# Four edits to a fused decoder layer on one core: another buffer for samples' states, an output tile issued earlier, weights split by one engine, and an end written out by hand

## Chip, core and metric

The kernel runs on one core of one Trainium2 chip. The metric is the device time of one execution in microseconds; lower is better. Before the change the median of three runs is 1122.03 us (1121.79 to 1123.79). The engines of the core are named as in the profile: PE is TensorE (matrix products), PEld its loading of weights, DVE is VectorE, ACT is ScalarE, POOL is GpSimd and SP is SyncE, which here does nothing but issue transfers.

## What is computed

One layer of a hybrid decoder in float32, for 512 tokens of one prompt and for 8 samples of 8 tokens each, with shared weights and a model width of 1024. The core of the reference:

```python
u = _rms(x) * g_pre_mix
z, xbc, dt_raw, q, k, v, ig, fg, og = jnp.split(u @ w_in, split_at, axis=-1)
xbc, conv_new = causal_conv(xbc, conv_buf, conv_w, conv_b)
...
y_ssd, h_new = ssd_scan(xs, dt, a, bm, cm, h_ssm)            # 16 heads, state 64 x 128 each
...
h_ml, c_new, n_new, m_new = mlstm_scan(q, k, v, i_pre, logf, mc, mn, mm)   # 4 heads, state 128 x 256
mix = jnp.concatenate([y_ssd, h_ml], axis=-1) @ w_out
x = x + _rms(mix) * g_post_mix
# cross-attention over 256 memory rows
x = x + _rms(o) * g_post_x
f = (jax.nn.silu(u @ w_gate) * (u @ w_up)) @ w_down          # hidden width 2816
x = x + _rms(f) * g_post_ffn
```

`_rms` divides by the root of the mean square plus 1e-6. The prompt starts from empty states; each sample brings its own states (`h0` for the SSD heads, `c0` for the mLSTM heads) and its own cached memory keys and values. Outputs are the layer's result (prompt and samples), the memory keys and values, and all states after the step.

## The kernel before

**Precision.** TensorE multiplies float32 in a reduced form, so every weight tile is split in two: `split_w` (L173) loads a 128x1024 piece `raw`, ScalarE casts it to `whi` (L181), and a low part `wlo = raw - whi` follows. Columns below `cut` are subtracted by VectorE (L188); those above go to GpSimd, either by a subtraction or, with `acc`, by ScalarE writing `-whi` into `wlo` (L185) and a transfer that GpSimd issues and that adds the raw weights from memory on top (L186). Each product is then three matmuls (L201 high by high, L202 high by low activation, L203 low weight by high activation). `raw` has two buffers, `whi` and `wlo` three each.

**Layout and stages.** Activations lie with features on the partitions and 576 tokens (512 prompt, 64 sample) along the free axis, in eight tiles of 128 features. The token axis is worked in two halves, 0 to 255 (`HALVES[0]`) and 256 to 575. The stages follow each other on TensorE: input projection (with the SSD scan and the mLSTM woven into it), values, gates, output projection, cross-attention, gated feed-forward, down projection.

**Who sets the order.** From the start to the output projection the framework's scheduler orders the instructions of each engine from their dependences and from the memory that tiles take and give back; `issue_after` adds a dependence by hand. Each engine works through its own queue in order; SP's queue holds most loads and the stores. From the cross-attention on a plan is written out by hand: functions are put at positions (`at_(position, function)`, L1424), sorted, and issued in that order on all engines (L1820 to L1822).

**Samples' SSD states (L651 to L735).** In four rounds `b`, two samples' states `h0` (128x1024) are loaded by SP (L714), read by eight products `ps_hs` (L718), scaled by `decs` on GpSimd (L725), updated from `ps_hu` (L728) by VectorE (L729) and stored (L731). They share the tag `t4` with the short-lived tiles `xdts` and `xes`: three buffers of 4 KB in a partition.

**Samples' mLSTM states (L897 to L925).** The same for `c0` in two groups of four samples: load (L912), four products `ps_nh` for the heads (L914) behind four of the group's own term (L907), update from `ps_cu` (L921), store (L924); again three buffers `t4`.

**Values (L756 to L794).** `gemm_tok` multiplies tokens by `wv` for the four heads, two weight pieces each; its third matmul is L777. It calls `split_w` with `acc`, so the upper 512 columns of the eight low parts come by L185 and L186. The results go to `vt4`, which takes all of slot 2 of the large buffers.

**Mixer's second half and output projection (L988 to L1150).** After the gates ScalarE and VectorE write the split of the mLSTM's half of the mixer's output (`mixm_h`, `mixm_l`) in eight tiles. The output projection runs in two passes: the first (`ps_o1`) over the SSD half, `mixs_h`, eight tiles; the second over `mixm_h`.

**The end (L1860 to L1918).** The down projection's last third is worked for half 1 of the tokens first, then for half 0 in eight tiles of 18 matmuls `ps_dn`. `down_evac` adds a tile to `f2` (VectorE, L1863), squares it (ScalarE, L266), adds the square to `ssqf` (VectorE, L267) and scales it (L1865). When half 1 is through, its inverse root mean square is formed (`rstd_cols`, L220: sums over the partitions by products with ones, L226; then on VectorE L236, a power on GpSimd L237, and a Newton step L238 to L240), spread to rows, applied to `f2`, added to the residual `x2` and stored (L1918). For half 0, `final0` transposes the residual (`ps_xt`) and `f2` (`ps_ft`) to token rows, both by L1876, copies the first to SBUF (L1884), and adds the scaled second: three of the four parts by VectorE (L1898), one by ScalarE and GpSimd (L1895, L1896). SP stores each part (L1899). In `final0` the order of TensorE alone is written by hand; other engines are left to the scheduler. L2020 is the end of the program: each engine's closing `DRAIN` and a barrier over all engines.

Of the kernel before, what the change touches and what calls it, by code (L numbers as in the profile page):

```python
# [19 lines left out]
P = 128  # L20
T = 576
# [95 lines left out]
def build(nc, tc, ctx, I, O):  # L117
# [178 lines left out]
    wz = ml.tile([P, 256], BF16, name="wz")  # L296
# [35 lines left out]
    st = ExitStack()  # L332
    sp = st.enter_context(tc.tile_pool(name="startp", bufs=1, reuse_waits="tile"))
# [48 lines left out]
    cdup = bcp.tile([16, 2, TS], F32, name="cdup")  # L382

# [182 lines left out]
    def ssd_prompt(g):  # L566
# [34 lines left out]
        for j in range(4):  # L601
# [3 lines left out]
            for k in range(2):  # L605
# [3 lines left out]
                lm = ml.tile([P, 512], F32, name="lm", tag="tmp", bufs=2)  # L609
# [70 lines left out]
    decs = sd.tile([P, 16, NB], F32, name="decs")  # L680
# [30 lines left out]
    for b in range(4):  # L711
        hns = [sd.tile([P, 16, 64], F32, name="h0", tag="t4", bufs=3) for _ in range(2)]
# [37 lines left out]
    vt4 = SL(2, "vt4", F32, (P, 4, 4, 258))  # L750
# [41 lines left out]
    for h in range(4):  # L792
        gemm_tok(I["wv"][h], U, UL, CHUNKS, v_evac(h), True)
# [5 lines left out]
    def head_norm(num, ex, n4, pool, name):  # L799

        ss = pool.tile([P, n4], F32, name="hn_ss", tag="hn_ss", bufs=2)
        jk = pool.tile([P, 256], F32, name="hn_jk", tag="hn_jk", bufs=1)
# [20 lines left out]
    for h in range(4):  # L823
# [38 lines left out]
        f = head_norm(num, expnm[:, :, h:h + 1].rearrange("p c o -> p (c o)"), 4, mp_, "p")  # L862
# [17 lines left out]
    es = ms.tile([P, 4, TS], F32, name="es")  # L880
# [21 lines left out]
    for hb in range(2):  # L902
# [31 lines left out]
        f = head_norm(num, ex, 1, ms, "s")  # L934
        hn = ms.tile([P, 256], F32, name="hns", tag="hns", bufs=1)
        V.tensor_scalar(hn, num[:, 0, 0:256], f, None, op0=ALU.mult)
# [8 lines left out]
    def tmp():  # L945
        return ml.tile([P, 512], F32, name="tmp", tag="tmp", bufs=2)
# [42 lines left out]
    ogs = ml.tile([P, KT, TS], F32, name="ogs")  # L989
# [87 lines left out]
    f = SL(5, "f_mix")  # L1077
# [7 lines left out]
    evs, ahead = [], []  # L1085
# [23 lines left out]
    for j in range(8):  # L1109
        gemm2([(*split_w(I["wout"][j, 0], cut=1024), KT)], act(mixs_h), act(mixs_l),  # L1110
              lambda t0, n, ps: evs.append(A.copy(f[:, j, t0:t0 + n], ps)), "ps_o1")
# [760 lines left out]
    def final0():  # L1872

        def rows(src, c, d, ps):
            for j in range(4):
                m = TE.transpose(ps[:, j * P:(j + 1) * P], src[:, 4 * d + j, c * P:(c + 1) * P], ident)  # L1876
            return ps.rearrange("p (j k) -> p j k", j=4), m

        parts = [(c, d) for c in range(2) for d in range(2)]
        xr = [wp.tile([P, 2, 4, P], F32, name="raw", tag="raw", bufs=2) for _ in range(2)]  # L1880
        xt = [xr[i // 2][:, i % 2] for i in range(4)]

        def put(i):
            A.copy(xt[i], rows(x2, *parts[i], (B1 if i == 3 else GP)("ps_xt"))[0])  # L1884

        with tc.manual_schedule(engines={TE.engine}):
            for i in range(3):
                put(i)
            rc = rstd_cols([ssqf], HCHUNKS[0], "pf0", alloc=B0)
            put(3)  # L1890
            ft = [rows(f2, *parts[i], (GP if i == 3 else MP)("ps_ft"))[0] for i in range(4)]
        for i, (c, d) in enumerate(parts):
            if i == 2:
                t = sw[:, 0:512].rearrange("p (j k) -> p j k", j=4)
                A.activation(t, ft[i], AF.Copy, scale=rc[:, c:c + 1])  # L1895
                G.tensor_tensor(xt[i], xt[i], t, op=ALU.add)  # L1896
            else:
                V.scalar_tensor_tensor(xt[i], ft[i], rc[:, c:c + 1], xt[i], op0=ALU.mult, op1=ALU.add)  # L1898
            S.dma_start(O["y0"][c, :, 4 * d:4 * d + 4, :], xt[i])  # L1899


    for n_, j in enumerate(range(8)):
        ps = (MP if n_ % 2 else GP)("ps_dn")[:, :256]
# [121 lines left out]
```

## Time and profile before

| | us |
|---|---|
| median of three runs | 1122.03 |
| lowest, highest run | 1121.79, 1123.79 |
| the profiled execution | 1122.92 |
| its span in the trace | 1121.2 |
| PE busy | 1100.6 |
| DVE busy | 703.7 |
| ACT busy | 594.3 |
| POOL busy | 223.0 |

The profiled execution is one run of its own; its span runs from its first to its last instruction. The granted clock of TensorE was 0.998 over it. In the rows of the prediction `L714` is line 714 of the kernel above; `out<-in` are tiles; `x8` is a count; `[2.10 <-DMA wlo<-wv]` says that the engine stood still for 2.10 us before the instruction and what released it. A timeline's first two columns are start and duration. A group's `min/median/max` are durations in ns. In the list of waits the numbers are the total in us, how many, and the longest.

### The profile page before, as it was taken

How to read it: one execution, taken by the hardware profiler on the slowest of the kernel's cores; microseconds unless marked ns; L12 is line 12 of the kernel's file. 1: busy time of each engine (PE TensorE's matmuls, PEld its weight loads, DVE VectorE, ACT ScalarE, POOL GpSimd, SP SyncE). 2: the span in 40 equal slices, each digit the busy share in tenths (PEclk: the TensorE clock that was granted, in tenths of full speed). 3: DMA queues.
4: the chain of work that ended last, by engine and by line, in shares of the span. 5: the costliest groups of instructions: out<-in, count | busy, mean ns of one | idle time of the engine just before them, and what ended most of it. 6: DMA issues, size and time to landing. Idle time of an engine off the chain costs nothing.

```text
span 1121.2 us, 21126 instructions
## 1 busy us (share of the span) xinstructions
PE 1100.6 (98%) x8423; PEld 1049.9 (94%) x8423; DVE 703.7 (63%) x1397; ACT 594.3 (53%) x1073; POOL 223.0 (20%) x300
## 2 busy tenths in 40 slices
PE   9999999899999999999999999999999999999996
PEld 8999889798998999999988889999999999999996
DVE  6796765557786775569654455776533665447555
ACT  6877533255563465656454445556435674246543
POOL 1333544313122121000144301101001110011001
PEclk9999999999999999999999999999999999999999
DMA  6685555626564447653567855745535774357532
GB/s 208 159 165 128 134 159 159 174 68 166 146 201 107 129 144 264 226 189 104 167 223 278 282 197 170 253 114 123 141 95 122 171 169 123 94 119 169 123 127 85
DMA packets 56231, 178.67 MB, mean 159 GB/s; under 512 B 6172, under 2 KB 10396, under 8 KB 55620
## 3 DMA queue, kind: packets, MB, share of 16 engines
q1 hardware_dynamic: 41732, 137.99, 37.8%
q0 software_dynamic: 14400, 39.33, 18.2%
q8 instruction: 66, 1.08, 0.4%
q14 instruction: 33, 0.27, 0.1%
HBM read 156.64 MB, written 20.65 MB: 158 GB/s over the span
## 4 chain that ended last, share of the span: by engine, by line
PE 89%; DMA 4%; DVE 2%; ACT 2%; issue 1%; POOL 1%; SPq 0%; DVEq 0%; POOLq 0%; ACTq 0%
PE ps_in L202 6%; PE ps_in L201 6%; PE ps_in L203 6%; PE ps_dn L203 4%; PE ps_dn L201 4%; PE ps_dn L202 4%; PE ps_o L203 3%; PE ps_o L202 3%; PE ps_o L201 3%; PE ps_g L1719 3%; PE ps_g L1720 3%; PE ps_g L1721 3%; PE ps_u L1719 3%; PE ps_u L1720 3%; PE ps_u L1721 3%; PE ps_v L777 2%
## 5 line engine op out<-in xcount | busy, mean ns | idle before, releaser
L181 ACT CAST whi<-raw 128x1024 fp32r<-128x1024 f32 x110 | 114.6, 1045 | 113.6 <-PE ps_dn L202 22.0
L202 PE MATMUL ps_in<-ul,whi 128*128 128x320 f32 (+1 forms) x544 | 164.3, 302 | 0.0
L201 PE MATMUL ps_in<-uh,whi 128*128 128x320 f32 (+1 forms) x544 | 163.9, 301 | 0.0
L203 PE MATMUL ps_in<-uh,wlo 128*128 128x320 f32 (+1 forms) x544 | 163.0, 300 | 0.5 <-DVE wlo L188 0.5
L188 DVE TENSOR_TENSOR wlo<-raw,whi 128x1024 fp32r<-128x1024 f32 (+1 forms) x102 | 102.8, 1009 | 82.0 <-ACT whi L181 81.2
L202 PEld LDWEIGHTS ps_in<-ul,whi 128*128 128x128 f32 x544 | 103.1, 190 | 2.5 <-issue 1.7
L201 PEld LDWEIGHTS ps_in<-uh,whi 128*128 128x128 f32 x544 | 103.1, 190 | 2.2 <-issue 1.3
L203 PEld LDWEIGHTS ps_in<-uh,wlo 128*128 128x128 f32 x544 | 103.1, 190 | 1.8 <-DVE wlo L188 0.7
L203 PE MATMUL ps_dn<-hh,wlo 128*128 128x320 f32 (+1 forms) x280 | 82.3, 296 | 0.8 <-DVE wlo L188 0.8
L201 PE MATMUL ps_dn<-hh,whi 128*128 128x320 f32 (+1 forms) x280 | 81.8, 296 | 0.6 <-ACT whi L181 0.5
L202 PE MATMUL ps_dn<-hl,whi 128*128 128x320 f32 (+1 forms) x280 | 82.0, 294 | 0.0
L203 PEld LDWEIGHTS ps_dn<-hh,wlo 128*128 128x128 f32 x280 | 52.5, 188 | 1.2 <-DVE wlo L188 1.2
L201 PEld LDWEIGHTS ps_dn<-hh,whi 128*128 128x128 f32 x280 | 52.3, 188 | 1.0 <-ACT whi L181 0.7
L202 PEld LDWEIGHTS ps_dn<-hl,whi 128*128 128x128 f32 x280 | 52.9, 189 | 0.0
L186 POOL DMA_DIRECT2D wlo<-win x32 | 27.9, 880 | 95.2 <-ACT wlo L185 89.2
L1719 PE MATMUL ps_u<-b,whi 128*128 128x288 f32 x144 | 42.5, 295 | 0.6 <-ACT ct L1751 0.6
L1720 PE MATMUL ps_u<-b,whi 128*128 128x288 f32 x144 | 42.5, 295 | 0.0
L1719 PE MATMUL ps_g<-b,whi 128*128 128x288 f32 x144 | 42.5, 295 | 0.0
L1720 PE MATMUL ps_g<-b,whi 128*128 128x288 f32 x144 | 42.5, 295 | 0.0
L777 PE MATMUL ps_v<-wlo,uh 128*128 128x256 f32 x128 | 36.5, 288 | 3.8 <-DMA wlo<-wv 3.8
L1671 POOL DMA_DIRECT2D wacc<-wgate x9 | 7.8, 871 | 159.4 <-ACT wacc L1670 147.1
L201 PE MATMUL ps_xo<-qh,whi 128*128 128x288 f32 x128 | 37.7, 300 | 1.0 <-ACT f_xo L1407 1.0
(720 smaller groups left out, 3681.3 us busy)
## 6 DMA issues: line engine op xcount, KB each, us to landing
raw<-win SPq DMA_DIRECT2D x35, 512.0 KB, 3.8
raw<-wout SPq DMA_DIRECT2D x17, 512.0 KB, 3.7
kva<-kc SPq DMA_DIRECT2D x16, 512.0 KB, 6.7
kva<-vc SPq DMA_DIRECT2D x16, 512.0 KB, 6.5
raw<-wdown SPq DMA_DIRECT2D x16, 512.0 KB, 3.6
raw<-wxq SPq DMA_DIRECT2D x13, 512.0 KB, 3.6
raw<-wgate SPq DMA_DIRECT2D x13, 512.0 KB, 3.6
raw<-wup SPq DMA_DIRECT2D x13, 512.0 KB, 5.1
```

Of the source, the lines that this page charges most:

```text
L181: A.copy(hi[:, :n], raw[:, :n])
L186: G.dma_start(lo[:, a:b], src[:, a:b], accum_op=ALU.add)
L188: e.tensor_tensor(lo[:, a:b], raw[:, a:b], hi[:, a:b].bitcast(F32), op=ALU.subtract)
L201: mm(ps, wh, ah, start=i == 0, stop=False)
L202: mm(ps, wh, al, start=False, stop=False)
L203: m = mm(ps, wl, ah, start=False, stop=i == len(tiles) - 1)
L777: m = mm(o, ah, lo[:, j:j + 256], start=False, stop=k == KT - 1, skip_group_check=True)
L1671: G.dma_start(out, s.src[j, :, c], accum_op=ALU.add)
L1719: mm(ps, wh, b[0][:, k, :], start=start and k == 0, stop=False, skip_group_check=True)
L1720: mm(ps, wh, b[1][:, k, :], start=False, stop=False, skip_group_check=True)
L1721: m = mm(ps, wl, b[0][:, k, :], start=False, stop=k == 3, skip_group_check=True)
```

## The change

Four edits come together.

1. The tag `t4` gets four buffers in place of three, for `h0` and for `c0`. The room comes from moves: `btk`, `decs` and later `es` are carved out of the slot of `vt4` (its tile is now allocated earlier, with 4608 columns); `cumst`, `ncum`, `wend`, `decp` move to `bcp`, `wz` to `startp`, `lm` to `ssds`, `tmp` and `ogs` to `zp`, and a scratch tile of `head_norm` is handed in (for the samples' rows it is the output tile itself).
2. The first tile of the output projection's first pass (`out1(0)`) is issued ahead of the splits `mixm_h`, `mixm_l`; from the fourth on, a split on ScalarE is issued after that tile's first copy.
3. `gemm_tok` takes `cut` in place of `acc`, and the values use 1024: the whole low part by VectorE.
4. From half 0 of the down projection on, all five engines follow a written plan. The residual's transposes stand among the last tiles' products. The square of the last tile is not added to `ssqf` but is a second term of the root's sums. The power on GpSimd becomes a root on ScalarE (`AF.Sqrt`) and a reciprocal on VectorE. Part 3 of the rows goes by ScalarE and VectorE, the other three by VectorE; ScalarE's queue issues the stores of parts 1 and 3. The residual of half 1 is added in four steps of two tiles.

```diff
-    cumst = ml.tile([80, T], BF16, name="cumst")
...
-    ncum = ml.tile([P, 4, 16], F32, name="ncum")
-    wend = ml.tile([P, 5, 16], F32, name="wend")
-    decp = ml.tile([P, 4, 16], F32, name="decp")
...
+    st = ExitStack()
+    sp = st.enter_context(tc.tile_pool(name="startp", bufs=1, reuse_waits="tile"))
+    wz = sp.tile([P, 256], BF16, name="wz")
...
+    cumst = bcp.tile([80, T], BF16, name="cumst")
+    ncum = bcp.tile([P, 4, 16], F32, name="ncum")
+    wend = bcp.tile([P, 5, 16], F32, name="wend")
+    decp = bcp.tile([P, 4, 16], F32, name="decp")
...
-                lm = ml.tile([P, 512], F32, name="lm", tag="tmp", bufs=2)
+                lm = sd.tile([P, 512], F32, name="lm", tag="tmp", bufs=2)
...
+    vt4_ = SL(2, "vt4", F32, (P, 4608))
     masks8 = C16("masks")[:TS, :].unsqueeze(1).to_broadcast([TS, 8, TS])
-    xdts = sd.tile([TS, 16, 64], F32, name="xdts", tag="t4", bufs=3)
-    xes = sd.tile([TS, 16, 64], F32, name="xes", tag="t4", bufs=3)
-    btk = sd.tile([TS, 2, P], F32, name="btk")
+    xdts = sd.tile([TS, 16, 64], F32, name="xdts", tag="t4", bufs=4)
+    xes = sd.tile([TS, 16, 64], F32, name="xes", tag="t4", bufs=4)
+    btk = vt4_[:TS, 4128:4384].rearrange("p (g k) -> p g k", g=2)
...
-    decs = sd.tile([P, 16, NB], F32, name="decs")
+    decs = vt4_[:, 4384:4512].rearrange("p (h b) -> p h b", h=16)
...
-        hns = [sd.tile([P, 16, 64], F32, name="h0", tag="t4", bufs=3) for _ in range(2)]
+        hns = [sd.tile([P, 16, 64], F32, name="h0", tag="t4", bufs=4) for _ in range(2)]
...
-    def gemm_tok(src, xh_, xl_, chunks, evac, acc=False, units=None):
-
-        units = units or [split_w(src[:, i, :], acc=acc) for i in range(2)]
+    def gemm_tok(src, xh_, xl_, chunks, evac, cut=CUT, units=None):
+        units = units or [split_w(src[:, i, :], cut=cut) for i in range(2)]
...
-        gemm_tok(I["wv"][h], U, UL, CHUNKS, v_evac(h), True)
+        gemm_tok(I["wv"][h], U, UL, CHUNKS, v_evac(h), 1024)
...
-    es = ms.tile([P, 4, TS], F32, name="es")
+    es = vt4_[:, 4128:4384].rearrange("p (h t) -> p h t", h=4)
...
-            c0 = ms.tile([P, 4, 258], F32, name="c0", tag="t4", bufs=3)
+            c0 = ms.tile([P, 4, 258], F32, name="c0", tag="t4", bufs=4)
...
-        return ml.tile([P, 512], F32, name="tmp", tag="tmp", bufs=2)
+        return zp.tile([P, 512], F32, name="tmp", tag="tmp", bufs=2)
...
+    f = SL(5, "f_mix")
+    evs = []
+    def out1(j):
+        gemm2([(*split_w(I["wout"][j, 0], cut=1024), KT)], act(mixs_h), act(mixs_l),
+              lambda t0, n, ps: evs.append(A.copy(f[:, j, t0:t0 + n], ps)), "ps_o1")
+    out1(0)
     for j in range(8):
         hm = qk[:, 4 * (j % 2) + j // 2, 0:TP]
-        A.activation(mixm_h[:, j, 0:TP], hm, AF.Copy, scale=ghalf[:, j:j + 1])
+        with tc.issue_after(evs[0].ins) if j > 2 else ExitStack():
+            A.activation(mixm_h[:, j, 0:TP], hm, AF.Copy, scale=ghalf[:, j:j + 1])
         V.scalar_tensor_tensor(mixm_l[:, j, 0:TP], hm, ghalf[:, j:j + 1], mixm_h[:, j, 0:TP].bitcast(F32),
                                op0=ALU.mult, op1=ALU.subtract)
...
-    for n_, j in enumerate(range(8)):
-        ps = (MP if n_ % 2 else GP)("ps_dn")[:, :256]
-        m = down_part(2, 6, j, 0, ps, w_of(j), 0, 6)
-        e = down_evac(n_, j, 0, ps, m)
-        if n_ == 0:
-            with tc.issue_after(m.ins):
-                rc = rstd_cols([ssqf], HCHUNKS[1], "pf1", alloc=B0)
-        if n_ == 1:
-            with tc.issue_after(m.ins):
-                rstd_rows(rc, HCHUNKS[1], rb, B0)
-        if n_ > 1:
-            ks = range(8)[:2] if n_ == 2 else range(8)[n_ - 1:n_] if n_ < 7 else range(6, 8)
-            for k in ks:
-                with tc.issue_after(e[1].ins):
-                    post_add(1, f2, x2, rb, [k], False)
-                if k % 2:
-                    S.dma_start(O["y1"][:, k - 1:k + 1, :], x2[:, k - 1:k + 1, 256:T])
-    final0()
+    plan = []
+    tail, squares = {}, {}
+    def root(name, terms, chunks):
+        n, ps = len(chunks), B0("ps_ss")
+        for c, (t0, _) in enumerate(chunks):
+            for m, (t_, b) in enumerate(terms):
+                mm(ps[:, c:c + 1], t_[:, t0 - b:t0 - b + P], ones, start=m == 0, stop=m == len(terms) - 1, skip_group_check=True)
+        v, y, a, r = [fp.tile([P, n], F32, name=name + k) for k in ("_v", "_y", "_a", "_r")]
+        tail[name] = v, y, a, r
+        V.tensor_scalar(v, ps[:, :n], 1.0 / 1024.0, EPS, op0=ALU.mult, op1=ALU.add)
+        A.activation(y, v, AF.Sqrt)
+    def root_end(name):
+        v, y, a, r = tail[name]
+        V.reciprocal(y, y)
+        V.tensor_tensor(a, y, y, op=ALU.mult)
+        V.scalar_tensor_tensor(a, a, -0.5, v, op0=ALU.mult, op1=ALU.mult)
+        V.scalar_tensor_tensor(r, a, 1.5, y, op0=ALU.add, op1=ALU.mult)
+        tail[name] = r
+    def root_rows1():
+        tail["ps"] = ps = B0("ps_rb")
+        for c, (t0, n) in enumerate(HCHUNKS[1]):
+            TE.transpose(ps[:, t0 - 256:t0 - 256 + n], tail["pf1"][:n, c:c + 1].to_broadcast([n, P]), ident[:n, :n])
+    def half0(j, k):
+        if k == 0:
+            tail[j] = (MP if j % 2 else GP)("ps_dn")[:, :256]
+        down_part(2, 6, j, 0, tail[j], w_of(j), k, k + 1)
+    def evac0(j):
+        fj = f2[:, j, 0:256]
+        V.tensor_tensor(fj, fj, tail[j], op=ALU.add)
+        if j:
+            squares[j] = ph.tile([P, 320], F32, name="sq", tag="sq", bufs=2)[:, :256]
+        A.activation(squares[j] if j else ssqf[:, 0:256], fj, AF.Square)
+        A.activation(fj, fj, AF.Copy, scale=PAR("g_postffn", j))
+    def sum0(j):
+        V.tensor_tensor(ssqf[:, 0:256], ssqf[:, 0:256], squares[j], op=ALU.add)
+    def resid1(q):
+        o, c = f2[:, 2 * q:2 * q + 2, 256:T], x2[:, 2 * q:2 * q + 2, 256:T]
+        V.tensor_tensor(o, o, rb[:, 256:T].unsqueeze(1).to_broadcast([P, 2, 320]), op=ALU.mult)
+        V.tensor_tensor(c, c, o, op=ALU.add)
+        S.dma_start(O["y1"][:, 2 * q:2 * q + 2, :], c)
+    for j in range(8):
+        for k in range(6):
+            at_(j + k / 6, half0, j, k)
+        at_(j + 1.03, evac0, j)
+        if 0 < j < 7:
+            at_(j + 1.45, sum0, j)
+    at_(0.99, root, "pf1", [(ssqf, 0)], HCHUNKS[1])
+    at_(1.9, root_end, "pf1")
+    at_(2.32, root_rows1)
+    at_(2.6, lambda: A.copy(rb[:, 256:T], tail["ps"][:, 0:320]))
+    for q, p in enumerate((2.95, 4.1, 5.1, 6.1)):
+        at_(p, resid1, q)
+    parts = [(c, d) for c in range(2) for d in range(2)]
+    xr, xt, ft = [], {}, {}
+    def token_rows(src, i, ps):
+        c, d = parts[i]
+        for j in range(4):
+            TE.transpose(ps[:, j * P:(j + 1) * P], src[:, 4 * d + j, c * P:(c + 1) * P], ident)
+        return ps.rearrange("p (j k) -> p j k", j=4)
+    def x_rows(i):
+        if i % 2 == 0:
+            xr.append(wp.tile([P, 2, 4, P], F32, name="raw", tag="raw", bufs=2))
+        xt[i] = xr[i // 2][:, i % 2], token_rows(x2, i, B1("ps_xt"))
+    def x_copy(i):
+        A.copy(*xt[i])
+    def f_rows(i):
+        ft[i] = token_rows(f2, i, (MP if i % 2 else GP)("ps_ft"))
+    def last(i):
+        o, rc = xt[i][0], tail["pf0"][:, parts[i][0]:parts[i][0] + 1]
+        V.scalar_tensor_tensor(o, ft[i], rc, o, op0=ALU.mult, op1=ALU.add)
+        store(i)
+    def store(i):
+        c, d = parts[i]
+        (A if i in (1, 3) else S).dma_start(O["y0"][c, :, 4 * d:4 * d + 4, :], xt[i][0])
+    def scaled():
+        tail["s"] = sw[:, 0:512].rearrange("p (j k) -> p j k", j=4)
+        A.activation(tail["s"], ft[3], AF.Copy, scale=tail["pf0"][:, parts[3][0]:parts[3][0] + 1])
+    def scaled_add():
+        V.tensor_tensor(xt[3][0], xt[3][0], tail["s"], op=ALU.add)
+        store(3)
+    for i in range(4):
+        at_(4.0 + i, x_rows, i)
+        at_(4.55 + i, x_copy, i)
+        at_(8.7 + i / 100, f_rows, i)
+    at_(8.4, lambda: root("pf0", [(ssqf, 0), (squares[7], 0)], HCHUNKS[0]))
+    at_(8.8, root_end, "pf0")
+    at_(9.0, scaled)
+    for i in range(3):
+        at_(9.01 + i / 100, last, i)
+    at_(9.1, scaled_add)
+    plan.sort()
+    with tc.manual_schedule(engines={TE.engine, A.engine, V.engine, G.engine, S.engine}):
+        for _, _, fn in plan:
+            fn()
```

More of the change, by code (lines that the diff above doesn't have):

```diff
@@ L331, in build @@
         w2 = split_w(I["win"][3], cut=1024)
-    st = ExitStack()
-    sp = st.enter_context(tc.tile_pool(name="startp", bufs=1, reuse_waits="tile"))
     ssqx = sp.tile([P, 640], F32, name="ssqx")
@@ L792, in build, with head_norm @@
     for h in range(4):
-        gemm_tok(I["wv"][h], U, UL, CHUNKS, v_evac(h), True)
+        gemm_tok(I["wv"][h], U, UL, CHUNKS, v_evac(h), 1024)
     st = ExitStack()
     mp_ = st.enter_context(tc.tile_pool(name="mlp", bufs=1, reuse_waits="tile"))
-    def head_norm(num, ex, n4, pool, name):
+    def head_norm(num, ex, n4, pool, jk):
         ss = pool.tile([P, n4], F32, name="hn_ss", tag="hn_ss", bufs=2)
-        jk = pool.tile([P, 256], F32, name="hn_jk", tag="hn_jk", bufs=1)
         for c in range(n4):
@@ L861, in build @@
             cprev = cn
-        f = head_norm(num, expnm[:, :, h:h + 1].rearrange("p c o -> p (c o)"), 4, mp_, "p")
+        f = head_norm(num, expnm[:, :, h:h + 1].rearrange("p c o -> p (c o)"), 4, mp_,
+                      mp_.tile([P, 256], F32, name="hn_jk", tag="hn_jk", bufs=1))
         S.dma_start(O["cp"][:, h, :], cprev[:, 0:257])
@@ L988, in build @@
     mixm_l = SL(4, "mixm_l", F32R)
-    ogs = ml.tile([P, KT, TS], F32, name="ogs")
+    ogs = zp.tile([P, KT, TS], F32, name="ogs")
     def og_evac(j):
@@ L1075, in weights @@
         return kept[-1][1]
-    f = SL(5, "f_mix")
     st = ExitStack()
@@ L1083, in build @@
     pre = dr.tile([P, len(PRE), 1024], F32, name="pre")
-    evs, ahead = [], []
+    ahead = []
     def presplit(n):
@@ L1109, in build @@
     for j in range(8):
-        gemm2([(*split_w(I["wout"][j, 0], cut=1024), KT)], act(mixs_h), act(mixs_l),
-              lambda t0, n, ps: evs.append(A.copy(f[:, j, t0:t0 + n], ps)), "ps_o1")
+        if j:
+            out1(j)
         presplit(min(len(turns), 1 if j else 2))
@@ L1870, in build @@
         S.dma_start(x2, x_d)
[L1872 to L1899, printed above, removed]
```

6 lines of the change are left out of this document (3 added, 3 removed).

## Prediction

> **What bounds the kernel now.** I read the page's busy times first, then busy time by stage, then TensorE's waits, then the stages that the change touches row by row.
>
> ```profile
> span 1121.2 us, 21126 instructions
> PE 1100.6 (98%) x8423; PEld 1049.9 (94%) x8423; DVE 703.7 (63%) x1397; ACT 594.3 (53%) x1073; POOL 223.0 (20%) x300
> 100.00:262.00 162.00, 157.97 (x1279) 141.97 (x1278) 100.45 (x192) 70.55 (x121) 64.73 (x73) 1.00 0.55 144
> 262.00:400.00 138.00, 138.00 (x1004) 127.41 (x1003) 105.11 (x290) 71.94 (x155) 31.41 (x42) 1.00 0.52 143
> 400.00:470.00 70.00, 70.00 (x526) 70.00 (x525) 43.16 (x58) 42.98 (x73) 11.46 (x19) 1.00 0.66 226
> 1070.00:1105.00 35.00, 34.91 (x261) 34.15 (x261) 21.26 (x47) 17.19 (x35) 0.87 (x1) 1.00 0.24 91
> 1105.00:1122.00 17.00, 6.63 (x57) 6.15 (x56) 8.06 (x22) 5.29 (x11) 2.07 (x2) 0.87 0.38 139
> PE ps_v L777 <- DMA wlo<-wv: 3.8, 2, 2.1
> PE ps_rb L251 <- ACT rxb L253: 1.5, 1, 1.5
> PE ps_ss L226 <- DVE ssqf L267: 1.1, 1, 1.1
> ```
>
> The first column after a window is its length, then TensorE, weight loads, VectorE, ScalarE, GpSimd. TensorE works through 1100.6 of 1121.2 us, so this kernel is a queue of matmuls: an edit pays only where TensorE stands still, where its order costs it time inside the busy figure, or behind its last matmul. The whole prize is 20.6 us. Of it the window 100 to 262 holds 4.0 (values, states of the samples), the windows 262 to 470 nothing, and the last window 10.4. The waits name the 4.0: 3.8 of them are two waits of the values' product for a low part brought by a DMA.
>
> **Part 1: a fourth buffer for the samples' states, and the tiles moved to make room.** No state's product (ps_hs, ps_nh) is among TensorE's waits at all, so there is no wait to remove: 0 by that. What the change does is to reorder. In the order of the built program TensorE's queue is the same up to the first sample group's state product; then the second group moves up by 104 places and the third and fourth follow.
>
> ```profile
> 146.07 1.06 PE L718 MATMUL ps_hs<-h,cpad 128*32 128x512 f32 x8
> 164.39 1.07 PE L718 MATMUL ps_hs<-h,cpad 128*32 128x512 f32 x8
> 142.55 0.33 SPq L714 DMA_DIRECT2D h<-h  x1
> 155.88 0.34 SPq L731 DMA_DIRECT2D o_ssms<-h  x1
> 159.49 0.34 SPq L714 DMA_DIRECT2D h<-h  x1
> L714 SPq DMA_DIRECT2D h<-h x8: 327/328/424, 113.1 to 202.3; - x8
> DMA to landing us min/median/max: 3.4/3.5/4.3
> ```
>
> The second group stood at 164.39, because its second state was issued only at 159.49, after the first state's store (155.88) had freed a buffer. In the new order it stands some ten matmuls behind the first group, at about 148.6 (an estimate: 146.07 + 1.06 + 10 products of 0.15). With a fourth buffer its second state takes the slot freed where 142.55 stands now; that load lands by 142.55 + 3.5 = 146.05, at the latest 146.85: 1.8 to 2.5 us in hand. SP's queue is in order: a load behind a store waits for the update that the store waits for, and the third and fourth groups' loads stand behind stores in both orders. I put 0.7 us of new waits there, between 0 and 3.0 (three groups, each late by one maximum over the median landing, 0.8, and a little more).
>
> The mixer's second half gains from the same reorder. TensorE's busy figure holds a cost wherever narrow products change place with wide ones:
>
> ```profile
> 273.77 0.62 PE L914 MATMUL ps_nh<-c,qpad 128*32 128x257 f32 x2
> 275.82 0.63 PE L914 MATMUL ps_nh<-c,qpad 128*32 128x257 f32 x6
> 276.70 1.07 PE L914 MATMUL ps_nh<-c,qpad 128*32 128x257 f32 x16
> ```
>
> A run of 16 takes 1.07 us, 0.067 each; a run of 2 takes 0.62 where 0.13 would do, a run of 6 takes 0.63 for 0.40. So breaking a group off costs 0.2 to 0.5 us. Before, a state's four heads are split 1 + 3 four times and the first-half term 3 + 1 once; in the new order all stand whole and three or four states follow one another. Five splits at 0.4 give 2.0 us, between 0 (the cost reappears at other borders) and 2.9 (each also slows the group behind it). I take -2.0.
>
> **Part 2: the output projection's first tile ahead of the splits of the mixer's second half.** The window 400 to 470 has TensorE busy for 70.00 of 70.00, so there is nothing to fill: 0. The same products are issued, in another order; ScalarE's splits after the third, which now wait for the first tile's copy, are used only by the second projection, seven tiles later. If that cover went, the queue behind the splits on ScalarE would hold up a copy out of PSUM; with 43 of 70 us busy it has room. Bounds 0 and +1.05 (one ScalarE cast, as the one at 210.54 below, in line ahead of such a copy).
>
> **Part 3: values' low parts by VectorE alone.** Before, a low part was half VectorE's (a subtraction of 512 columns) and half a chain: ScalarE writes minus the high part, GpSimd issues a DMA that adds the raw weights to it.
>
> ```profile
> 187.40 2.00 ACT L181 CAST whi<-raw 128x1024 fp32r<-128x1024 f32 x2
> 193.27 1.18 POOL L186 DMA_DIRECT2D wlo<-wv  x1
> 199.64 0.39 PE L777 MATMUL ps_v<-wlo,uh 128*128 128x256 f32 x1 [2.10 <-DMA wlo<-wv]
> 210.54 1.05 ACT L181 CAST whi<-raw 128x1024 fp32r<-128x1024 f32 x1
> 217.68 0.28 PE L767 MATMUL ps_v<-whi,uh 128*128 128x256 f32 x1
> 188.48 1.51 DVE L188 TENSOR_TENSOR wlo<-raw,whi 128x512 fp32r<-128x512 f32 x1 [3.95 <-ACT whi L181]
> L188 DVE TENSOR_TENSOR wlo<-raw,whi x102: 676/1217/1721, 19.0 to 1060.3; 128x1024 fp32r<-128x1024 f32 x52, 128x512 fp32r<-128x512 f32 x49, 128x768 fp32r<-128x768 f32 x1
> 185.61 3.83 POOL L725 TENSOR_TENSOR h<-h,decs 128x1024 f32<-128x1024 f32 x2
> ```
>
> It takes 8 ScalarE instructions, 8 GpSimd DMA issues and 8 transfers away, and makes eight subtractions of 512 columns into 1024: 1.22 us each (the median of the row, whose largest group has that width) for 0.68 (its minimum), 8 x 0.54 = 4.3 us more on an engine that is busy for 100 of 162 us. The cover: the cast that a waiting product needs ended at 189.4 and at 211.6; TensorE came to the product at about 197.5 and 217.8. One or two subtractions of 1.2 us are over by 192 and 213, 5 us ahead. They may be slower: beside GpSimd's product (185.61 to 189.44) the 512-column form took 1.51, so up to 1.72 in the row, 2.5 times its minimum; at that rate 1024 columns take 3.1, and two in line still end at 195.6, the single one at 214.7. So both waits go: -3.8, with 0 as the other end.
>
> On this the Trainium skill ("SBUF — State Buffer", section "Who interferes with whom") has a rule that speaks against the edit: a VectorE instruction with two SBUF operands and a GpSimd one that reads SBUF take turns at one port pair, and the loser stands for the whole of the other. By that a subtraction that meets one GpSimd product of 1.9 takes 3.1, and the sum stays; if each of the two met two of them, they would end at 189.4 + 10.0 = 199.4, as late as the DMA was, and the sum would be 1.9 smaller. The stretch of 1.51 against 0.68 agrees in sign.
>
> **Part 4: the written end.** It is a chain behind the last matmul of ps_dn:
>
> ```profile
> 1107.19 0.28 PE L203 MATMUL ps_dn<-hh,wlo 128*128 128x256 f32 x1
> 1107.31 1.47 PE L1876 MATMUL ps_xt<-c,x 128*128 128x128 f32 x12
> 1107.59 0.41 DVE L1863 TENSOR_TENSOR f_ffn<-f_ffn,ps_dn 128x256 f32<-128x256 f32 x1
> 1108.90 0.43 ACT L266 ACTIVATE sq<-f_ffn 128x256 f32<-128x256 f32 x1
> 1109.85 0.60 PE L226 MATMUL ps_ss<-c,ssqf 128*128 128x1 f32 x4 [1.07 <-DVE ssqf L267]
> 1110.92 0.15 DVE L236 TENSOR_SCALAR pf_v<-ps_ss 128x2 f32<-128x2 f32 x1
> 1111.21 0.81 POOL L237 TENSOR_TENSOR pf_y<-pf_v,c 128x2 f32<-128x2 f32 x1 [14.26 <-DVE pf_v L236]
> 1112.73 2.07 DVE L1898 SCALAR_TENSOR_TENSOR raw<-ps_ft,pf_r,raw 128x512 f32<-128x512 f32 x3
> L1899 SPq DMA_DIRECT2D o_y<-raw x4: 332/345/438, 1113.5 to 1115.1; - x4
> L2020 POOLq DRAIN  x3: 46/93/6939, 1113.4 to 1120.9; - x3
> L2020 SPq DRAIN  x3: 7/7/7, 1117.8 to 1120.6; - x3
> ```
>
> Before: from the last product's start (1107.19) to the span's end 14.0 us. SP has seen its stores land at 1117.8, but GpSimd's closing DRAIN began at 1113.4 and took 6.94, to 1120.4; the other engines wait for it. After: 16 x transposes move in front, 16 x 0.12 = +1.9 ahead of the last product. Behind it: addition done at +0.8 (1107.59 + 0.41); the square at once instead of 0.9 later, done at +1.3; no addition to the sum of squares but two more root products (0.3, as half of the four at 0.60), so the root's first VectorE step comes at 1.3 + 1.07 + 0.3 = +2.7. A ScalarE root and a reciprocal (0.2 and 0.2, estimates by VectorE's 0.15) in place of GpSimd's 0.81, then three small steps as before: first scaled rows at +4.0 (before: 1112.73, +5.5). Three of 0.69, then a fourth addition of 0.69: +6.8; the last store is issued and lands 2.7 later (1115.1 to 1117.8): +9.5. GpSimd has no instruction left in the written end, so its DRAIN runs out early; the closing barrier takes 0.8 (1120.4 to 1121.2): +10.3. With the 1.9 that is 12.2 against 14.0: -1.8. SP's own landing is no earlier than before (7.19 + 1.9 + 9.5 = 1118.6): the gain is the DRAIN, and without that there is none. Bounds -3.0 (all but 0.7 of the added work hidden) and +0.9 (below).
>
> The root needs a table load on ScalarE, placed in the first root where half 1 ends.
>
> ```profile
> L440 ACT ACT_TABLE_LOAD x4 | 5.1, 1283 | 0.1
> ```
>
> It is 1.28 us on an idle ScalarE. Between that root and the transposes of its result stand 1.33 tiles of 18 products at 0.12, 2.9 us of matmuls; root (1.4) and small steps (1.2) take 2.6, and with the load in line 3.9: up to 1.0 us of stall, 0 if it is fetched while the sums come in. It is within the 0.7 of new waits. By the Trainium skill ("ScalarE: Activation LUTs", section "Rules for kernel authors") a switch of set is to be budgeted at about 2.7 us; the row has 1.28, and by the page's figure the term would grow by 1.4.
>
> **The sum.** The profiled execution took 1122.92 us, its span 1121.2 and 1.7 around it; it is 0.9 above the runs' median of 1122.03. -3.8 (values' waits) - 2.0 (regrouped products) + 0.7 (new waits) - 1.8 (end) = -6.9: 1116.0 for an execution like the profiled one, 1115.1 by the median. I say **1115.1**.
>
> **Rivals.**
> - *The end gains nothing* (chance 0.12). GpSimd's DRAIN may not follow its last instruction but the stores: it ended 1120.4, 2.6 after they landed. For it: it is long only at the end. Against: it began before the stores were issued. Then the end runs to +9.5 + 2.6 + 0.8 + 1.9 = 14.8, +0.8 over before, and the sum is -4.3: 1117.7.
> - *The waits on the values come back* (0.10): a VectorE with 4.3 us more to do, its queue in order behind additions that wait for PSUM, brings the low parts as late as the DMA did. For: 1.51 for 0.68. Against: 2 to 5 us in hand. It gives 3.8 back: 1118.9.
> - *Slower* (0.08): the moved-up second group stands in front of TensorE's queue for a state whose buffer isn't free. If the load keeps its place after the first state's store has landed (159.49 + 3.5 = 163.0), TensorE stands from 148.6 to 163.0, 14.4 us: -6.9 + 14.4 = +7.5, 1129.5. It decides above 9.1 us of stall. Against: the buffer is one that the mixer's short rows free, by 142.55.
> - *No change* (0.10): the reorder from 148 us on costs in small waits and borders what the waits gave (+3.0 and 0 for -2.0 and +0.7), and the end is a wash: -3.8 + 3.0 = -0.8, 1121.2.
>
> **How the numbers follow.** Forecast 0.60. Its own range, from the bounds, is 1112 (-3.8 - 2.9 - 3.0 = -9.7) to 1118 (regrouping worth nothing, the end 1.0: -4.1). To leave out no more than 2 in 10, the range goes to 1119.5 above, over the first two rivals: 1111.5 to 1119.5. A change under 0.2%, 2.2 us, can't be told from none. Faster: 0.60 + 0.12 + 0.10 = 0.82; same 0.10; slower 0.08.
>
> **What would show it.** The wait of ps_v for a DMA is gone from TensorE's waits and none for wlo by VectorE stands there; the window 100 to 262 loses its 4 us. No ps_hs or ps_nh among the waits (a ps_hs over 1 us: the slower rival). The ps_nh products stand in runs of 16 and more, and TensorE's busy total falls by about 2 us. GpSimd's closing DRAIN ends before SP's, and the span ends within 1 us of the last store's landing; if that DRAIN still ends it, the first rival holds.

## The result and the profile after

The changed kernel takes 1114.59 us (median of four runs, 1114.35 to 1115.19); the kernel before 1122.91 (the three runs of above and one more beside the changed kernel, 1121.79 to 1124.12). The ratio is 0.9925, with a 95% interval of 0.9913 to 0.9937: faster by 0.75%, clear of 0.2%. The forecast was 1115.1. The profiled execution took 1114.63 with a span of 1112.9, 8.3 less than before.

First the page's head, TensorE's waits and the busy time by stage of the kernel after (columns as before):

```profile
span 1112.9 us, 21074 instructions
PE 1097.6 (99%) x8427; PEld 1050.7 (94%) x8427; DVE 707.3 (64%) x1391; ACT 591.1 (53%) x1068; POOL 213.3 (19%) x289
PE ps_rb L251 <- ACT rxb L253: 1.3, 1, 1.3
PE ps_o L201 <- ACT f_mix L1014: 1.1, 1, 1.1
PE ps_hu L729 <- DVE h L730: 1.1, 1, 1.1
PE ps_ss L1891 <- ACT sq L1920: 0.8, 1, 0.8
100.00:262.00 162.00, 160.78 (x1305) 145.15 (x1303) 107.35 (x199) 69.48 (x119) 63.09 (x71) 1.00 0.47 139
262.00:400.00 138.00, 136.91 (x1024) 129.64 (x1023) 110.41 (x296) 75.48 (x161) 27.86 (x36) 1.00 0.48 137
400.00:470.00 70.00, 70.00 (x526) 70.00 (x525) 38.62 (x51) 39.65 (x68) 9.79 (x19) 1.00 0.68 234
```

The wait of the values' product for its transfer has gone, and no wait for the low part by VectorE took its place. In their stead stand two waits that the kernel before did not have, 1.1 us each: `ps_hu` in the first window and `ps_o` in the second, which had no idle time before. TensorE is busy for 3.0 us less in all and idle for 15.3 in place of 20.6.

The state products in the timeline (start, duration):

```profile
148.40 1.07 PE L719 MATMUL ps_hs<-h,cpad 128*32 128x512 f32 x8
270.63 0.64 PE L915 MATMUL ps_nh<-c,qpad 128*32 128x257 f32 x8
272.82 1.51 PE L915 MATMUL ps_nh<-c,qpad 128*32 128x257 f32 x24
320.63 1.94 PE L915 MATMUL ps_nh<-c,qpad 128*32 128x257 f32 x32
```

The second group of `ps_hs` moved to 148.40 and did not wait. `ps_nh` runs in 8, 24 and 32: no state is split any more, and in the run of 32 a product costs 0.061 us (1.94 / 32). What is paid is the number of runs more than the number of products: in these traces runs of 2, 6 and 8 take 0.62 to 0.64 us alike. In all, `ps_nh` keeps TensorE busy for 5.2 us in place of 8.3.

The end, from the last product of `ps_dn`, and the closing instructions of the program (durations there in ns):

```profile
1103.08 0.28 PE L203 MATMUL ps_dn<-hh,wlo 128*128 128x256 f32 x1
1104.33 0.38 PE L1891 MATMUL ps_ss<-c,sq 128*128 128x1 f32 x2 [0.85 <-ACT sq L1920]
1105.20 0.16 DVE L1894 TENSOR_SCALAR pf_v<-ps_ss 128x2 f32<-128x2 f32 x1 [1.37 <-PE ps_ss L1891]
...
1106.49 2.07 DVE L1967 SCALAR_TENSOR_TENSOR raw<-ps_ft,pf_r,raw 128x512 f32<-128x512 f32 x3
L2097 POOLq DRAIN  x3: 93/180/7887, 1044.2 to 1112.4; - x3
L2097 SPq DRAIN  x3: 7/7/7, 1111.6 to 1111.9; - x3
```

(The line `...` stands for lines left out.) From 1103.08 to the span's end are 9.8 us, 14.0 before. GpSimd's long DRAIN, 7.9 us, began at 1044.2, behind GpSimd's last transfer, and was over 59 us before anybody needed it. SP sees the last store landed at 1111.6; 1.3 us later the span ends.

### The profile page after: what moved, and what is told of

It reads as the page before. It is cut to its first block, busy times and chain, and to the rows that moved or that the text cites. A ratio compares the mean times of both kernels' runs of the same rounds, so it can differ in the third digit from the quotient of the medians.

```text
span 1112.9 us, 21074 instructions
## 1 busy us (share of the span) xinstructions
PE 1097.6 (99%) x8427; PEld 1050.7 (94%) x8427; DVE 707.3 (64%) x1391; ACT 591.1 (53%) x1068; POOL 213.3 (19%) x289
## 4 chain that ended last, share of the span: by engine, by line
PE 92%; DMA 2%; DVE 2%; ACT 2%; issue 1%; SPq 0%; DVEq 0%; ACTq 0%
PE ps_in L201 6%; PE ps_in L202 6%; PE ps_in L203 6%; PE ps_dn L201 4%; PE ps_dn L203 4%; PE ps_dn L202 4%; PE ps_o L201 3%; PE ps_o L203 3%; PE ps_o L202 3%; PE ps_g L1729 3%; PE ps_g L1730 3%; PE ps_g L1731 3%; PE ps_u L1729 3%; PE ps_u L1730 3%; PE ps_u L1731 3%; PE ps_v L778 2%
## 5 line engine op out<-in xcount | busy, mean ns | idle before, releaser
L188 DVE TENSOR_TENSOR wlo<-raw,whi 128x1024 fp32r<-128x1024 f32 (+1 forms) x102 | 107.4, 1055 | 81.3 <-ACT whi L181 80.4
L201 PE MATMUL ps_o<-mixs_h,whi 128*128 128x320 f32 (+1 forms) x128 | 38.3, 299 | 1.1 <-ACT f_mix L1014 1.1
```

Source lines behind the costliest of these rows:

```text
L188: e.tensor_tensor(lo[:, a:b], raw[:, a:b], hi[:, a:b].bitcast(F32), op=ALU.subtract)
L201: mm(ps, wh, ah, start=i == 0, stop=False)
```

## The experiments

Every kernel was profiled once and timed in rounds against the kernel before on the same chip. Up to eighteen products from the first `ps_hs` on, TensorE's order is the same in all of them; the time to the first `ps_hs` still differs by up to 1.3 us from trace to trace, so the table also gives the span counted from there. The changed kernel was measured twice and differs by 0.6 us in the median and 0.3 counted so; less than that is not read. The last column is the stretch from the first `ps_hs` to the last `ps_o`, the end of the output projection. It repeats far better: TensorE's order in it is the same for the changed kernel, its repeat and runs 1 and 2, and they differ by 0.1 us.

| kernel | median us | ratio to before (95%) | span | first ps_hs | from there to the end | from there to the last ps_o |
|---|---|---|---|---|---|---|
| before | 1122.91 | | 1121.2 | 146.07 | 975.1 | 360.0 |
| changed | 1114.59 | 0.9925 (0.9913 to 0.9937) | 1112.9 | 145.66 | 967.2 | 354.0 |
| changed, again | 1115.20 | 0.9922 (0.9909 to 0.9935) | 1113.4 | 145.93 | 967.5 | 354.0 |
| 1 a late GpSimd copy | 1117.43 | 0.9949 (0.9933 to 0.9965) | 1116.0 | 146.07 | 969.9 | 354.1 |
| 2 the end of before | 1115.84 | 0.9932 (0.9918 to 0.9945) | 1114.5 | 145.33 | 969.1 | 354.0 |
| 3 values as before | 1123.24 | 0.9996 (0.9986 to 1.0006) | 1122.8 | 145.75 | 977.0 | 363.7 |
| 4 first tile back | 1116.43 | 0.9938 (0.9923 to 0.9953) | 1114.7 | 146.28 | 968.4 | 355.1 |
| 5 three buffers | 1116.24 | 0.9936 (0.9922 to 0.9950) | 1114.2 | 145.43 | 968.7 | 355.7 |
| 6 four for c0 alone | 1114.60 | 0.9921 (0.9908 to 0.9934) | 1113.4 | 146.14 | 967.3 | 353.9 |
| 7 four for h0 alone | 1118.84 | 0.9959 (0.9946 to 0.9972) | 1117.1 | 146.25 | 970.8 | 357.6 |
| 8 other PSUM banks | 1113.47 | 0.9910 (0.9896 to 0.9924) | 1111.9 | 146.67 | 965.2 | 352.7 |
| 8 again | 1114.07 | 0.9914 (0.9901 to 0.9927) | 1111.3 | 146.19 | 965.1 | 352.7 |
| 9 before, values alone | 1117.98 | 0.9948 (0.9934 to 0.9962) | 1115.3 | 145.86 | 969.4 | 355.4 |
| 10 banks and c0 alone | 1113.24 | 0.9906 (0.9892 to 0.9920) | 1110.9 | 145.35 | 965.5 | 353.1 |

Of the kernels set against the changed one only runs 3 and 7 have intervals clear of its two; every timed execution of runs 1, 2 and 5 is also longer than its longest (1115.57). Differences of 1 to 2 us are therefore read from the traces.

**1. A late GpSimd copy: is it the DRAIN?**

```diff
     at_(9.1, scaled_add)
+    late = fp.tile([P, 2], F32, name="late")
+    at_(9.2, lambda: G.tensor_copy(late, xt[3][0][:, 0, 0:2]))
```

> The changed kernel with one GpSimd copy of 128x2 behind the last addition of the end; nothing else waits for it. Theory (the end's gain is that GpSimd's closing DRAIN, 5.6 to 7.9 us from its last instruction, is over early): the DRAIN now begins near 1109 and ends the span again, 1109.2 + 5.6 to 7.9 + 0.8, so 1115.6 to 1117.9 against 1112.9: 2.7 to 5.0 us longer, with GpSimd's DRAIN ending after SP's. Rival (the DRAIN follows the stores, or its length is nobody's wait): span within 0.3 us of the changed kernel.

GpSimd's timeline and the closing instructions of this run:

```profile
1109.76 0.18 POOL L1994 COPY late<-raw 128x2 f32<-128x2 f32 x1 [64.20 <-DVE raw L1980]
L2099 POOLq DRAIN  x3: 46/93/5191, 1109.7 to 1115.7; - x3
L2099 SPq DRAIN  x3: 7/7/7, 1112.1 to 1115.2; - x3
```

A copy of 0.18 us that nothing reads makes the kernel 2.7 us longer, at the lower end of what was expected: the DRAIN behind it takes 5.2 us, to 1114.9, while SP had its stores at 1112.1. The rival by which the DRAIN follows the stores falls; it follows GpSimd's last instruction.

**2. The end of before.** `final0` and the loop around it in place of the written plan.

> The changed kernel with the end of before (final0, order of TensorE alone by hand); the other three edits stay. Theory: 2.3 us longer than the changed kernel, 1.9 less of matmuls ahead of the last product and 14.0 us behind it in place of 9.8; GpSimd's DRAIN ends the span. Rival (the end is worth nothing, the gain came ahead of it): within 0.5 us of the changed kernel. Neither: over 3.5 us, the written order of half 0 then also saves waits that the list does not show.

2.0 us longer, 1.3 by the medians (0.6 against the changed kernel's second median). GpSimd's DRAIN of 6.3 us from 1107.4 ends the span again:

```profile
L2031 POOLq DRAIN  x3: 46/93/6287, 1107.4 to 1114.2; - x3
```

Not all of the 2.0 is the end's. Behind the last `ps_dn` stand 13.3 us in place of the changed kernel's 9.8; from the first `ps_dn` to the last it takes 304.2 us in place of 306.3, as the transposes are not there. That makes 1.4 for the end. The other 0.6 lies between the last `ps_o` and the first `ps_dn`, a stretch that the edit leaves alone.

**3. Values' low parts as before.**

```diff
-        gemm_tok(I["wv"][h], U, UL, CHUNKS, v_evac(h), 1024)
+        gemm_tok(I["wv"][h], U, UL, CHUNKS, v_evac(h), True)
```

with `gemm_tok` passing `acc` on as before.

> The changed kernel with the values' upper low parts by ScalarE and a transfer that adds, as before. Theory: the waits of ps_v for that transfer come back, 3.8 us in two, so 1118.4; VectorE's shorter subtractions (4.3 us less) may shorten the new wait of ps_hu (1.1) and give 2.7 at least. Rival (in the new order the values' products stand later and the transfer is in time): within 0.5 us of the changed kernel.

Neither: 9.8 us longer (8.0 and 8.7 against the two medians of the changed kernel), the whole gain of the change gone. One of the two waits for the transfer comes back, with 1.2 us in place of 3.8, and TensorE's largest wait is now another one. The largest three new rows in the list of waits, the place of the first, and the loads of the SSD states (L715) and the stores (L732) between 140 and 215 us in this run:

```profile
PE ps_hs L719 <- DMA h<-h: 5.3, 1, 5.3
PE ps_v L768 <- DVE vts L789: 1.3, 1, 1.3
PE ps_v L778 <- DMA wlo<-wv: 1.2, 1, 1.2
178.59 1.93 PE L719 MATMUL ps_hs<-h,cpad 128*32 128x512 f32 x8 [5.33 <-DMA h<-h]
L715 SPq DMA_DIRECT2D h<-h x5: 327/328/332, 142.2 to 191.8; - x5
DMA to landing us min/median/max: 6.2/6.2/6.2
L732 SPq DMA_DIRECT2D o_ssms<-h x8: 332/343/344, 156.9 to 212.2; - x8
DMA to landing us min/median/max: 2.6/7.2/8.3
```

and the same two lines of the kernel in the changed kernel's trace:

```profile
L715 SPq DMA_DIRECT2D h<-h x5: 328/328/338, 142.2 to 185.5; - x5
DMA to landing us min/median/max: 3.5/3.5/3.5
L732 SPq DMA_DIRECT2D o_ssms<-h x8: 332/343/344, 157.3 to 204.1; - x8
DMA to landing us min/median/max: 2.9/4.6/4.7
```

A buffer of a state comes round in one store and one load: 4.6 + 3.5 = 8.1 us without the adding transfers, 7.2 + 6.2 = 13.4 with them (medians). The third group of `ps_hs` stands in TensorE's queue for that. The stop costs more than its 5.3 us: behind it the granted clock is 0.50 from 176 to 182 us, the eight products of `ps_hs` take 1.93 us in place of 1.06, and the next ones of `ps_v` start 0.21 us apart in place of 0.12, about 1.6 us in all (an estimate from these spacings). Behind the two waits of the kernel before, 2.1 us at most, the granted clock stayed at 1.00. It is the third rival of the prediction, one group later than it was placed; what keeps the changed kernel from it is part 3.

**4. The projection's first tile back behind the splits.**

```diff
-    out1(0)
     for j in range(8):
         hm = qk[:, 4 * (j % 2) + j // 2, 0:TP]
-        with tc.issue_after(evs[0].ins) if j > 2 else ExitStack():
+        if True:
             A.activation(mixm_h[:, j, 0:TP], hm, AF.Copy, scale=ghalf[:, j:j + 1])
...
     for j in range(8):
-        if j:
-            out1(j)
+        out1(j)
```

> The changed kernel with the output projection's first tile back behind the mixer's splits, and no split made to wait for its copy. Theory (the move adds the wait of ps_o for the copy of f_mix, 1.09 us at 398.4, and hides nothing): 1.1 us shorter, 1113.5, that wait gone. Rival (the move covers the head transposes ps_ht or the splits, and without it TensorE waits for mixs_h or the last head): the same or up to 3 us longer, with a wait of ps_o or ps_ht in the list.

1.2 us longer (1.8 in the medians), 1.1 of it before the last `ps_o`: the theory falls. ScalarE's and TensorE's timelines in the changed kernel, and here:

```profile
394.47 1.94 ACT L1020 ACTIVATE mixm_h<-qk,ghalf 128x512 fp32r<-128x512 f32 x3
397.04 1.07 ACT L871 COPY qk<-ps_ht 128x512 f32<-128x512 f32 x2 [0.62 <-PE ps_ht L870]
398.00 0.39 ACT L1014 COPY f_mix<-ps_o 128x256 f32<-128x256 f32 x1
398.44 0.41 PE L201 MATMUL ps_o<-mixs_h,whi 128*128 128x320 f32 x1 [1.09 <-ACT f_mix L1014]
```

```profile
395.09 3.79 ACT L1019 ACTIVATE mixm_h<-qk,ghalf 128x512 fp32r<-128x512 f32 x6
398.78 1.05 ACT L871 COPY qk<-ps_ht 128x512 f32<-128x512 f32 x2
399.72 0.37 ACT L1014 COPY f_mix<-ps_o 128x256 f32<-128x256 f32 x1
400.14 0.41 PE L201 MATMUL ps_o<-mixs_h,whi 128*128 128x320 f32 x1 [2.18 <-ACT f_mix L1014]
```

The wait is not made by part 2 but halved by it. The copy that frees a PSUM bank stands behind three splits in the changed kernel and behind six here, and TensorE stands for 2.18 us in place of 1.09. On TensorE nothing moved: the two traces have the same products in the same order, all 8427. What part 2 changes is ScalarE's order; whether by the tile's place in the program or by the splits that must wait for its copy, no run separates.

**5 to 7. Which states need the fourth buffer.** `bufs=4` of the tag `t4` set to 3 for both kinds (5), for `xdts`, `xes` and `h0` alone (6), for `c0` alone (7).

> The changed kernel with three buffers t4 for both kinds of states; the tiles stay where the change put them. Theory (the fourth buffer pays by whole groups of ps_nh, -2.6 us in the two traces, and costs a new wait of ps_hu, 1.1): 1.5 to 3 us longer than the changed kernel, ps_nh again split, no wait of ps_hu. Rival (the moved tiles, not the buffer, changed the order): within 0.5 us.

> Four buffers for the mLSTM states alone, three for the SSD states. Theory (the second group of ps_hs moved up brings four GpSimd products back to back, 146.8 to 156.3, beside which VectorE's two products of lm took 4.62 us and a subtraction 2.55, and that makes the wait of ps_hu): the wait goes, ps_nh keeps its whole groups, 1.1 us shorter than the changed kernel or down to 0. Rival (the SSD states' buffer gains as well): 0.5 to 2 us longer.

> Four buffers for the SSD states alone, three for the mLSTM states. Theory: ps_nh is split again and its 2.6 us come back, the wait of ps_hu stays: 2 to 3 us longer than the changed kernel. Rival (the scheduler groups ps_nh by other things than the buffers): within 0.5 us.

With three for both it is 1.5 us longer, with four for `c0` alone as fast as the changed kernel, with four for `h0` alone 3.6 longer, and 2.1 longer than with three for both. So what the fourth buffer gives comes from `c0`, and for `h0` it gives nothing. What the moves of tiles cost or give, which all three runs keep, no run shows. `ps_nh` in run 7 and in run 6 (some of its rows):

```profile
315.23 0.64 PE L915 MATMUL ps_nh<-c,qpad 128*32 128x257 f32 x6
316.42 1.05 PE L915 MATMUL ps_nh<-c,qpad 128*32 128x257 f32 x10
318.04 0.64 PE L915 MATMUL ps_nh<-c,qpad 128*32 128x257 f32 x8
```

```profile
267.37 1.51 PE L915 MATMUL ps_nh<-c,qpad 128*32 128x257 f32 x24
269.12 0.62 PE L915 MATMUL ps_nh<-c,qpad 128*32 128x257 f32 x2
316.25 1.93 PE L915 MATMUL ps_nh<-c,qpad 128*32 128x257 f32 x30
```

The split groups are back in run 7, and in part in run 6 too, against what was expected of it: `ps_nh` keeps TensorE busy for 7.9 us in run 5, 6.5 in run 6, 8.1 in run 7 and 5.2 in the changed kernel.

Why `h0`'s buffer cost the wait of `ps_hu`: GpSimd's, VectorE's and TensorE's timelines of the changed kernel.

```profile
146.82 9.50 POOL L726 TENSOR_TENSOR h<-h,vt 128x1024 f32<-128x1024 f32 x4 [2.59 <-PE ps_hs L719]
147.03 4.62 DVE L614 TENSOR_TENSOR lm<-lm,cbs 128x512 f32<-128x512 f32 x2
151.98 2.55 DVE L188 TENSOR_TENSOR wlo<-raw,whi 128x1024 fp32r<-128x1024 f32 x1
154.45 0.67 DVE L730 TENSOR_TENSOR h<-h,ps_hu 128x512 f32<-128x512 f32 x1
155.27 0.47 PE L729 MATMUL ps_hu<-stb,bm 96*128 96x512 f32 x1 [1.09 <-DVE h L730]
```

The earlier group gives GpSimd four products in a row instead of two. Beside them two products of VectorE took 4.62 us and a low part 2.55; the addition that frees the bank of `ps_hu` came at 154.45. In run 6 the same engines show:

```profile
147.31 4.29 POOL L726 TENSOR_TENSOR h<-h,vt 128x1024 f32<-128x1024 f32 x2 [2.60 <-PE ps_hs L719]
147.51 4.64 DVE L614 TENSOR_TENSOR lm<-lm,cbs 128x512 f32<-128x512 f32 x2
152.47 1.21 DVE L188 TENSOR_TENSOR wlo<-raw,whi 128x1024 fp32r<-128x1024 f32 x1
```

With two GpSimd products the two of VectorE are as slow, but the low part behind them takes 1.21, and the wait is not in the list, as expected. That the long low part made the wait is read from these rows; run 6 also takes back the earlier group, so it does not test that alone. TensorE is busy for 1.3 us more in run 6 (1098.9 against 1097.6) by another order, so nothing is left of the wait.

**8. The first tile in the other PSUM banks.**

```diff
-    out1(0)
+    out1(0, MP)
```

where `out1` hands its second argument to `gemm2` as `alloc`.

> The changed kernel with the output projection's first tile in the other group of PSUM banks, so that it need not wait for the banks that the gates' last tile and its own first half hold. Theory: the wait of 1.09 us at 398.4 goes and nothing takes its place, 1113.5. Rival (the wait moves to the second tile, since ScalarE is late with the copies and not the banks scarce): within 0.3 us of the changed kernel, with the wait on a later ps_o.

> The changed kernel itself beside the next two, so that they are compared on one chip: 1114.6, within 0.7 us.

> The changed kernel with the projection's first tile in the other PSUM banks, a second time beside the changed kernel: 1.0 us shorter than it, the wait of ps_o for f_mix gone.

The wait of `ps_o` is gone both times. By the medians it is 1.1 us shorter both times; counted from the first `ps_hs` 2.0 and 2.4, of which 1.1 are that wait and 0.6 a wait of `ps_sa` for its load, which is in the changed kernel's list and not in these. Up to the last `ps_o` both are 1.35 us shorter. The intervals of the ratios overlap.

**9. The values alone, in the kernel before.** The edit of part 3 and nothing else.

> The kernel before with the values' low parts by VectorE alone, nothing else. Theory (undoing this in the changed kernel cost 9.8 us because the adding transfers also stretch the states' loads, 3.5 to 6.2 us, in an order that now stands on them; in the order of before only the two waits of ps_v hang on them): 3.8 us shorter than before, both waits gone, 1118. Rival (the transfers cost the kernel before as much elsewhere): 6 us shorter or more. Other rival (VectorE late with the low parts): under 2 us shorter, a wait of ps_v for wlo by VectorE.

Both waits are gone and none came; 5.9 us off the span, 5.6 off the median beside it, 5.7 counted from the first `ps_hs`. Of the 5.7, 4.6 come before the last `ps_o`, 3.8 of them by the two waits; 0.65 is a shorter DRAIN at the end (6.29 us in place of 6.94), which the edit does not touch; the last 0.4 lies between the last `ps_o` and the end and stays open, as does the 0.8 beside the waits. Without the DRAIN it is 5.0, between the theory and the first rival.

**10. Other banks, and the fourth buffer for c0 alone.**

> Other banks and the fourth buffer for the mLSTM states alone. Theory: each takes its wait away (ps_o 1.09, ps_hu 1.09), but the run with the fourth buffer for the mLSTM states alone already had neither, and gave 1.6 back in product time by another order; so the two don't add: between the changed kernel and 1.0 us shorter. Rival (they add): 2 us shorter.

1113.24 us beside 1115.20 for the changed kernel on the same chip, 2.0 less: more than the theory allowed, but no more than the banks alone gave counted from the first `ps_hs` (965.5 against 965.1 and 965.2), so they do not add. TensorE is busy for 352.99 of the 353.22 us from the first state product to the memory keys:

```profile
145.35:498.57 353.22, 352.99 (x2711) 333.32 (x2711) 243.98 (x527) 176.37 (x336) 77.76 (x91) 1.00 0.51 160
```

It has the lowest median measured, with the fourth buffer only where it pays. But up to the last `ps_o` the one with other banks alone is 0.4 us ahead of it (352.7 against 353.1); which of the two is faster, these runs do not tell.

## Why the prediction was right

The mechanisms were the forecast's own, and the change was somewhat larger: 8.3 us, by the medians and by the traces, for a forecast of 6.9. That the time came within 0.5 us is in part luck: it was counted from 1122.03, and the median of the kernel before rose to 1122.91 with one more run. By stages, up to the last `ps_o` the changed kernel won 5.9 us (forecast: -3.8 - 2.0 + 0.7 = -5.1) and at the end 2.1 (forecast 1.8); 0.4 came before the first `ps_hs`, where nothing was to be won, and 0.1 was lost in between. Inside the 5.9 two terms were mis-sized and their errors met.

- **Values' waits, -3.8: right.** The two waits went and VectorE was in time; run 9 shows it by itself. The rival of late low parts falls, though its mechanism is real: beside GpSimd's products one low part of 1024 columns took VectorE 2.55 us, and 1.21 in run 6 where they had ended. That agrees in kind with the Trainium skill ("SBUF — State Buffer", section "Who interferes with whom"), by which a VectorE instruction with two SBUF inputs and a GpSimd instruction that reads SBUF take turns; the price fell on `ps_hu`, not on the values.
- **Regrouped state products and new waits, together -1.3: measured -1.5** by run 5. The sum was right and is `c0`'s, as the argument by split groups had it; both sizes were too small. Against run 5 TensorE is busy for 3.2 us less (1097.6 against 1100.8, 2.7 of it in `ps_nh`) where 2.0 were forecast, and waits 1.7 more, 1.1 at `ps_hu` and 0.6 at `ps_o`, where 0.7 were. The new waits were looked for at `ps_hs` behind a load, where none came; they are for results that VectorE and ScalarE had yet to read out of PSUM.
- **The projection's first tile, 0: mis-sized, measured -1.1** by run 4, up to the last `ps_o`. The step read the window 400 to 470 of the kernel before as it stood, full. But the projection now begins near 393 in place of 402, with the mixer's splits still ahead of it on ScalarE; there their order matters. The part named the right queue and the right price (a copy out of PSUM behind a split, up to 1.05) but charged it to the move, which relieves it.
- **The end, -1.8: measured -2.1** between the two traces: 2.1 us more from the first `ps_dn` to the last (forecast 1.9), 4.2 less behind it, 9.8 us where 10.3 were forecast. Run 2 gives 1.4; its DRAIN happened to be 0.65 shorter than that of the kernel before. As worked out, the stores land no earlier: 10.6 us behind the last `ps_dn` before, 8.5 and 2.1 of transposes ahead now. The gain is that the span ends 1.3 us behind the landing (forecast: within 1) and not 3.4, and run 1 shows the reason. The table load of 1.28 us lay on an idle ScalarE, as said, and no wait of the rows' transposes came.
- **The slower rival** does not happen in the changed kernel but does in run 3: with the adding transfers still there, nearly the same order waits 5.3 us for a state and gives back all that was won. The prediction gave it 0.08 because it took the transfers' end for a matter of the values alone. The parts don't add: part 3 alone gave 5.7 us (0.65 of it the DRAIN's), and taken back it cost 9.8.

## What to carry to other kernels

Price an edit against the order in which the other edits leave the queues, not against the trace of before: what stands ahead of one copy on ScalarE, worth nothing in a full window, was worth 1.1 us once the stage had moved up by 9. A buffer that lets products of one kind run whole pays even where nothing waits for it, and can cost where it only bunches work on an engine that slows another; try it for each user by itself. Compare traces stage by stage where TensorE's order is the same: the stretch repeats within 0.1 us where the whole time does within 0.6. And look behind the last store: here GpSimd's closing DRAIN counted from its own last instruction and was the long one, so GpSimd should finish early.

## What was not expected of the hardware

GpSimd's closing DRAIN is recorded from the start of GpSimd's last instruction. It took 5.2 us behind a copy of 0.18 (run 1), 6.3, 6.3 and 6.9 behind an addition of 1.26 (runs 2 and 9, the kernel before), and 7.8 to 8.6 behind a transfer that GpSimd issued; from the end of the copy or addition that is 5.0, 5.0, 5.0 and 5.6. That of SP took 0.007. Why it is so long stays open.

Beside the adding transfers of 256 KB that GpSimd issues, SP's loads of 512 KB took 6.2 us in place of 3.5 and its stores 7.2 in place of 4.6 (medians) in the same stretch, while the DMA engines moved a mean of 155 GB/s there, against 146 without them.

And behind a stop of 5.3 us TensorE ran at a granted clock of 0.50 for some 6 us (run 3).
